# Two of the first branch's projections with tokens on the partitions, the compressed-key product in one rounded pass, and four warming products left out

## The chip, the cores and the metric

One core of a Trainium2 chip runs the whole program. The metric is the device time in microseconds (us) of one execution. Three runs of the kernel before gave 501.91, 502.08 and 502.62 us; their median, 502.08 us, is the time before.

## The reference, cut to what matters

The input x has 256 tokens of 1024 channels. It is normalised and modulated by a vector c (through `w_ada`) into h, and one wide projection `h @ w_in + b_in` feeds three parallel branches, which are mixed by sigmoid gates and projected once more. Cut to the parts that the change touches:

```
proj = h @ w_in[l] + b_in[l]
(aq, ak, av, ao, az, ai, af, ba, bb, bz, cq, ckc, cvc, cks, cvs, ckw, cvw, cg, cz, mg) = split_cols(proj)
# branch a: mLSTM heads over aq, ak, av, then a normalisation per head, and two gates
hf = (hf - mu) * rsqrt(mean((hf - mu)**2) + 1e-5)
hn = hf.reshape(b, s, W_A) * mlstm_norm[l]
y_a = sigmoid(ao) * hn * silu(az)
# branch b: gated causal convolution of 31 taps, layer norm, silu, gate bz
# branch c: attention over three key sets (compressed, selected, window) with gates per head
p_c = masked_softmax(s_c, ...);  o_c = einsum('bgjqn,bngd->bqgjd', p_c, vc)      # 15 compressed blocks
y_c = (gb0 * o_c + gb1 * o_s + gb2 * o_w) * silu(cz)
merged = g0 * (y_a @ w_branch[l, 0]) + g1 * (y_b @ w_branch[l, 1]) + g2 * (y_c @ w_branch[l, 2])
out = x + gate * rmsnorm(merged @ w_out[l], norm_post[l])
```

## The kernel before, in words

All weights are float32 in HBM. For TensorE a float32 operand is split into two rounded parts (`float32r`), hi and lo, and a product becomes three: hi by hi, lo by hi, hi by lo. ScalarE casts the weights to hi (`w_hi`), VectorE subtracts to get lo (`w_lo`); both are in `split` (line 370). Weights come in half megabytes through rings of three hi and three lo tiles and four raw tiles, in the fixed order of the list `order` (line 376); `part` keeps two halves ahead of TensorE. All loads go out on SyncE's queue. Smaller products (attention scores, transposes, attention's products with values) stay in plain float32.

The input projection has two forms. `feat` (line 640) puts output features on the partitions: the weights are the stationary operand, and the 256 tokens the moving one, so that 128 features take 24 products of 256 columns; ScalarE takes each result out with its bias. `tok` (line 660) puts 128 tokens on the partitions: h is stationary, 512 weight columns are the moving operand, and 512 features of 256 tokens take 48 products of 512 columns into two PSUM banks; VectorE takes each result out and adds a bias row that was loaded to all partitions (`vb_av`, `vb_mg`). The kernel before uses `tok` for av, cvs with cvw, and mg, and `feat` for the rest, az and ao among them.

The order of work is written by a planner while the program is built. `Loom` keeps a model clock of each engine and issues every instruction in one program order. Side work is a list of generators (`spawn`, with a rank) that `weave` (line 216) steps between products of the projection when the model says that their operands are ready; `until`, `room`, `slot` and `calm` yield the model time from which a step may go. The 31-tap convolution (`conv_gen`, line 704) is the filler: `weave` issues its VectorE steps only while VectorE's model queue is less than 600 ns ahead of TensorE. `need` forces a generator to its end.

In time: a first wave over the 8 slices of D (lines 515 to 610), whose weights and modulation arrive together; the projections of branch c's keys and queries; per head `h` of four the groups aq, ak, av, az, bz with the head's cell woven in, and the attention (`nsa_gen`, line 1002) woven in across them; then ao and cz; then the branch products c, a, b, each after its mg gates; then the output product.

Attention, per group `g` and token half `t`, ends in a loop (line 1101) that transposes the probabilities in blocks of 128 keys (`flips`), copies them out of PSUM on ScalarE, and multiplies them with the values into one PSUM bank `po`. The compressed keys are the last block: 16 rows of `ptc` (the other 112 are zero) against `vcmp`, one plain float32 product over all 128 rows. Branch a ends in `hnorm_gen` (line 1163): VectorE scales the head's output (`num`, tokens on partitions), TensorE transposes it into `ps_ht`, VectorE multiplies by the gate `ga` (features on partitions, silu(az) times sigmoid(ao) times `anorm`), and `ysplit` (line 772) makes hi on ScalarE and lo on VectorE.

`heat` (line 325) multiplies a tile of ones with itself for no result; `HEAT` gives 10 such products at the start and 4 just ahead of the first wave (line 562).

Of the kernel before, what the change touches and what calls it, by code (L numbers as in the profile page):

```python
# [17 lines left out]
S = 256  # L18
D = 1024
# [16 lines left out]
VROW = ("av", "cv", "mg")  # L36
COLS = dict(av=("av",), cv=("cvs", "cvw"), mg=("mg",))

ORDER = [(n, 0) for n in ("ckc", "cvc", "cks", "ckw")] + [("cv", 0), ("cv", 1)] + [("cq", i) for i in range(4)]
for _i in range(H_A):  # L40
    ORDER += [("aq", _i), ("ak", _i)]
    if _i % 2 == 0:
        ORDER += [("av", _i), ("av", _i + 1)]
    ORDER += [("az", _i), ("bz", _i)]
# [4 lines left out]
VB_MG = 1024 + 512 + N_MISC  # L49

# [13 lines left out]
HEAT = (10, 4)  # L64
# [212 lines left out]
def trunk(ctx: ExitStack, tc, xtok, wada, wave0, wgrp, wmisc, w1, wbr, wout, par, vbias, out):  # L277
# [98 lines left out]
    order = []  # L376
    for n, i in ORDER:
        if n != "mg":
            order.append(("wgrp", (GROUP[n, i],), 2, 1))
# [437 lines left out]
    vcmp = [const.tile([128, 128], F32, name=f"vcmp{g}") for g in range(2)]  # L817
    for g in range(2):
        pool.memset(vcmp[g], 0.0)

    def cmp_gen(j):
# [59 lines left out]
        else:  # L881
            for g in range(2):
# [5 lines left out]
                act.copy(vcmp[g][0:16, :], ps[0:16, 0:128])  # L888
# [113 lines left out]
    def nsa_gen(qs, oc, ptc):  # L1002
        for g in range(2):
            for t in range(2):
# [74 lines left out]
                yield from loom.slot("sd", 2)  # L1079
                po = bank("ps_o", "sd")  # L1080
# [4 lines left out]
                def flips(c, kind, kt):  # L1085
# [6 lines left out]
                    if kind == 2:  # L1092
                        act.copy(ptc[0:16, :], pt[0:16, :])
                        drop(pt)
                        return vcmp[g], ptc
# [4 lines left out]

                ops = yield from flips(*blocks[0])
                for b in range(len(blocks)):
                    v, p_t = ops
                    if b + 1 < len(blocks):
                        ops = yield from flips(*blocks[b + 1])
                    yield until("pe", p_t)
                    mm(po, v, p_t, b == 0, b == len(blocks) - 1)
# [55 lines left out]
    def hnorm_gen(num, ga):  # L1163
# [10 lines left out]
        dve.tensor_tensor(f, f, v3, op=OP.mult)  # L1174
        for h in range(4):
            for t in range(2):
                hn = num[:, 2 * h + t]
                dve.tensor_scalar(hn, hn, mv[:, h, t, 0:1], f[:, h, t:t + 1], op0=OP.subtract, op1=OP.mult)
            yield until("pe", num)
# [5 lines left out]
            gg = ga[:, 2 * h:2 * h + 2]  # L1185
            yield until("dve", pt)
            dve.tensor_tensor(gg, pt.rearrange("p (i q) -> p i q", i=2), gg, op=OP.mult)
# [26 lines left out]
    ptc = const.tile([128, 512], F32, name="ptc")  # L1214
    pool.memset(ptc, 0.0)
# [9 lines left out]
    def silu_gen(h, *deps):  # L1225
        yield from loom.after(*deps)
        for z in (ga, zb):
            if h < 3:
                yield from loom.calm("act", z[:, 2 * h:2 * h + 2])
            act.activation(z[:, 2 * h:2 * h + 2], z[:, 2 * h:2 * h + 2], AF.Silu)  # L1230
# [3 lines left out]
    ga = bigt("ga")  # L1234
    zb = bigt("zb")
    for h in range(4):
# [21 lines left out]
        group_feat("az", h, evac_fn(lambda t: ga[:, t]))  # L1258
# [5 lines left out]
    def gated(t, s, y, scale=None):  # L1264
        if y is ga:
            yield from loom.after(*g_silu)
        yield until("dve", s)
        if scale is None:
            dve.tensor_tensor(y[:, t], y[:, t], s, op=OP.mult)
        else:  # L1270
            dve.scalar_tensor_tensor(y[:, t], y[:, t], scale, s, op0=OP.mult, op1=OP.mult)
# [4 lines left out]
    def evac_cz(t, ps, b):  # L1276
# [4 lines left out]
        late_.append(spawn(gated(t, s, oc), 1))  # L1281

    def evac_ao(t, ps, b):
        if len(late_) > 1:
            need(late_[-2])
        s = ringt(work, [128, S], "sz", "t256", 2)
        act.activation(s, ps, AF.Sigmoid, bias=b)
        late_.append(spawn(gated(t, s, ga, pc("anorm", t)), 1))

    for i in range(4):  # L1290
        group_feat("ao", i, evac_ao)
# [3 lines left out]
    def split_c():  # L1295
        for k in range(0, KT, 2):
            while len(late_) < 10 + k:
                yield loom.now() + 300
            yield from loom.after(*late_[8 + k:10 + k])
# [13 lines left out]
    def branch_a():  # L1313
# [3 lines left out]
        for k in range(0, KT, 2):  # L1317
            yield from ysplit(ga, y_hi, y_lo, k)
# [140 lines left out]
def pack(x, c, w_ada, b_ada, norm_pre, norm_post, w_in, b_in, mlstm_conv_w, mlstm_conv_b, mlstm_norm, conf_dw_w,  # L1459
# [71 lines left out]
    rows = [b_in[OFF[n]:OFF[n] + SIZES[n]] for n in ("av", "cvs", "cvw")] + [bm, b_in[OFF["mg"]:OFF["mg"] + SIZES["mg"]]]  # L1531
# [17 lines left out]
```

## Time and profile before

| | us |
|---|---|
| median of three runs | 502.08 |
| profiled execution, its own time | 502.75 |
| its span, first to last instruction | 501.0 |
| TensorE products / VectorE / ScalarE busy in it | 491.0 / 431.8 / 303.1 |

The profiled execution took 502.75 us, of which 1.75 us lie outside its span. Busy times are of instructions as recorded, and a product is recorded from its issue until its pipeline is through, so that neighbouring products overlap; the share of busy time of TensorE says how rarely it had nothing in hand, and the chain of waits gives the time per product. Nearly all instructions carry line 174, the line of the helper that records them, and so are told apart by their tiles. TensorE's clock was granted in full (1.00) in every stretch up to 494 us.

### The profile page before, as it was taken

What the parts mean: (1) busy time and instruction counts of PE and PEld (TensorE: products, weight loads), DVE (VectorE), ACT (ScalarE), POOL (GpSimd) and SP (SyncE); (2) the same over time, 40 slices, a digit from 0 to 9 for tenths busy, and PEclk for the clock granted to TensorE, in tenths of its full rate; (3) what the DMA queues carried; (4) which work ended last, traced back from release to release, by engine and by line L of the source; (5) the groups of instructions that cost most, each with busy time, mean ns of one, the idle gap of its engine ahead of it and who ended that gap; (6) DMA issues with size and microseconds to landing.
All of it is one profiled execution on the core that took longest, in us unless ns stands there. A gap on an engine that the chain in (4) does not pass through costs nothing.

```text
span 501.0 us, 8523 instructions
## 1 busy us (share of the span) xinstructions
PE 491.0 (98%) x3237; PEld 436.4 (87%) x3237; DVE 431.8 (86%) x871; ACT 303.1 (61%) x519; POOL 7.3 (1%) x41
## 2 busy tenths in 40 slices
PE   8999999999999999999999999999999999999994
PEld 8999998799878989978899799997888788888883
DVE  4989899999999899999999996679998986656745
ACT  6556756245464975977749775666656844454442
POOL 5000000000000000000000000000000000000000
PEclk9999999999999999999999999999999999999998
DMA  8999964884776262232424426554387686655402
GB/s 297 409 359 375 406 244 150 318 352 146 284 285 238 95 241 86 96 156 86 169 84 169 169 84 219 194 208 179 96 317 291 200 354 236 243 220 186 169 0 84
DMA packets 18784, 106.38 MB, mean 212 GB/s; under 512 B 2220, under 2 KB 2616, under 8 KB 8632
## 3 DMA queue, kind: packets, MB, share of 16 engines
q1 hardware_dynamic: 18600, 105.82, 56.0%
q8 instruction: 25, 0.41, 0.3%
q14 instruction: 15, 0.12, 0.1%
q10 hardware_dynamic: 144, 0.03, 0.0%
HBM read 104.78 MB, written 1.06 MB: 211 GB/s over the span
## 4 chain that ended last, share of the span: by engine, by line
PE 83%; DVE 11%; DMA 2%; issue 2%; ACT 1%; SPq 0%; DVEq 0%; ACTq 0%
PE ps_f L174 30%; PE ps_t L174 28%; PE w L174 9%; PE ps_out L174 4%; DVE w_lo L174 4%; DVE acc L174 3%; PE ps_o L174 3%; PE ps_s L174 2%; PE ps_p L174 1%; DMA a_raw<-in_wada_dram 1%; DMA w_raw<-in_w_dram 1%; PE ps_qk L174 1%; PE ps_n L174 1%; PE ps_c L174 1%; DVE cm L174 1%
## 5 line engine op out<-in xcount | busy, mean ns | idle before, releaser
L174 DVE TENSOR_TENSOR w_lo<-w_raw,w_hi 128x1024 fp32r<-128x1024 f32 (+1 forms) x150 | 180.0, 1205 | 40.6 <-ACT w_hi L174 39.2
L174 ACT CAST w_hi<-w_raw 128x1024 fp32r<-128x1024 f32 (+1 forms) x150 | 154.9, 1034 | 81.9 <-PE ps_t L174 53.3
L174 PE MATMUL ps_f<-h_hi,w_hi 128*128 128x256 f32 x512 | 130.7, 291 | 0.0
L174 PE MATMUL ps_f<-h_lo,w_hi 128*128 128x256 f32 x512 | 126.3, 283 | 0.0
L174 PEld LDWEIGHTS ps_f<-h_hi,w_hi 128*128 128x128 f32 x512 | 98.0, 191 | 2.5 <-issue 2.0
L174 PEld LDWEIGHTS ps_f<-h_lo,w_hi 128*128 128x128 f32 x512 | 98.1, 192 | 1.4 <-issue 1.0
L174 DVE SCALAR_TENSOR_TENSOR acc<-u,p_sb,acc 128x226 f32<-128x226 f32 (+28 forms) x232 | 93.0, 460 | 1.8 <-ACT acc L174 1.6
L174 PE MATMUL ps_f<-h_hi,w_lo 128*128 128x256 f32 x512 | 75.7, 288 | 0.0
L174 PEld LDWEIGHTS ps_f<-h_hi,w_lo 128*128 128x128 f32 x512 | 67.0, 191 | 2.6 <-issue 1.9
L174 PE MATMUL ps_t<-w_hi,h_hi 128*128 128x512 f32 x144 | 58.2, 404 | 0.2 <-DVE gs L174 0.2
L174 PE MATMUL ps_t<-w_hi,h_lo 128*128 128x512 f32 x144 | 56.2, 391 | 0.0
L174 PE MATMUL ps_t<-w_lo,h_hi 128*128 128x512 f32 x144 | 44.8, 392 | 0.0
L174 PEld LDWEIGHTS ps_t<-w_hi,h_hi 128*128 128x128 f32 x144 | 27.1, 188 | 6.3 <-DVE gs L174 0.7
L174 PEld LDWEIGHTS ps_t<-w_lo,h_hi 128*128 128x128 f32 x144 | 26.8, 188 | 6.4 <-issue 0.8
L174 PEld LDWEIGHTS ps_t<-w_hi,h_lo 128*128 128x128 f32 x144 | 27.1, 188 | 5.2 <-issue 0.2
L174 PE MATMUL w<-h_lo,w_hi 128*128 128x256 f32 x128 | 31.5, 284 | 0.0
L174 PE MATMUL w<-h_hi,w_lo 128*128 128x256 f32 x128 | 31.4, 283 | 0.0
L174 DVE SCALAR_TENSOR_TENSOR a_raw<-a_raw,cb 128x1024 f32<-128x1024 f32 x23 | 27.4, 1218 | 0.2 <-DMA a_raw<-in_wada_dram 0.2
L174 ACT ACT_TABLE_LOAD x20 | 25.7, 1283 | 1.5 <-PEq L1541 1.2
L174 PEld LDWEIGHTS w<-h_lo,w_hi 128*128 128x128 f32 x128 | 24.5, 191 | 0.1
L174 PEld LDWEIGHTS w<-h_hi,w_lo 128*128 128x128 f32 x128 | 24.5, 192 | 0.0
L174 ACT ACTIVATE pm<-pm,mx 128x16 f32<-128x16 f32 (+2 forms) x48 | 19.0, 400 | 1.9 <-DVE mx L174 1.9
(265 smaller groups left out, 695.5 us busy)
## 6 DMA issues: line engine op xcount, KB each, us to landing
w_raw<-in_wgrp_dram SPq DMA_DIRECT2D x50, 1024.0 KB, 4.9
w_raw<-in_wbr_dram SPq DMA_DIRECT2D x12, 1024.0 KB, 4.8
a_raw<-in_wada_dram SPq DMA_DIRECT2D x16, 512.0 KB, 7.7
w_raw<-in_w_dram SPq DMA_DIRECT2D x8, 1024.0 KB, 4.9
w_raw<-in_wave_dram SPq DMA_DIRECT2D x14, 512.0 KB, 7.0
a_raw<-in_wada_dram SPq DMA_DIRECT2D x4, 1024.0 KB, 4.9
w_raw<-in_wout_dram SPq DMA_DIRECT2D x4, 1024.0 KB, 4.8
vb_mg<-in_vbias_dram SPq DMA_DIRECT2D x3, 512.0 KB, 5.6
```

Source lines behind the costliest of these rows:

```text
L174: inst = self.pin(fn(*args, **kw))
```

## The change

az and ao join the projections with tokens on the partitions: az as two groups, in the passes h = 1 and h = 3, and ao as two groups ahead of cz. Their bias rows are two more loads of 512 KB to all partitions, in the ring of two that holds `vb_av` and `vb_mg`. VectorE now takes both out of PSUM. The gate `ga` is kept with tokens on the partitions, so that in `hnorm_gen` the scaling goes to ScalarE (with a bias `nb`, minus mean times factor) and the gate is multiplied ahead of the transposes; behind them, `hsplit_gen` has ScalarE scale by `anorm` and round to hi, and VectorE form lo, both out of PSUM.

`ptc` and `vcmp` become `float32r` with three bands of 16 rows: hi, lo, hi of the probabilities against hi, hi, lo of the values, so that one rounded product of 512 columns gives the sum of three. The block is transposed first and multiplied last, and the bank `po` is taken only at the first product.

`HEAT`'s second number is 0: the four products ahead of the first wave are left out.

```diff
@@ -33,20 +33,24 @@
-VROW = ("av", "cv", "mg")
-COLS = dict(av=("av",), cv=("cvs", "cvw"), mg=("mg",))
+VROW = ("av", "cv", "az", "ao", "mg")
+COLS = dict(av=("av",), cv=("cvs", "cvw"), az=("az",), ao=("ao",), mg=("mg",))
-    ORDER += [("az", _i), ("bz", _i)]
+    else:
+        ORDER += [("az", _i - 1), ("az", _i)]
+    ORDER += [("bz", _i)]
+VB_AZ = VB_MG + 3 * D
+VB_AO = VB_AZ + D
@@ -61,7 +65,7 @@
-HEAT = (10, 4)
+HEAT = (10, 0)
@@ -374,7 +378,16 @@
+    vb_a = {}
+
+    def load_vb_a(n):
+        vb_a[n] = vbt("vb_" + n)
+        at = VB_AZ if n == "az" else VB_AO
+        loom.load(nc.sync, vb_a[n], vbias[:, at:at + D].broadcast_to([128, D]))
+
+        if n in ("az", "ao") and i == 0:
+            order.append(lambda n=n: load_vb_a(n))
@@ -814,9 +827,9 @@
-    vcmp = [const.tile([128, 128], F32, name=f"vcmp{g}") for g in range(2)]
+    vcmp = [const.tile([128, 128], F32R, name=f"vcmp{g}") for g in range(2)]
-        pool.memset(vcmp[g], 0.0)
+        pool.memset(vcmp[g].bitcast(F32), 0.0)
@@ -885,7 +898,10 @@
-                act.copy(vcmp[g][0:16, :], ps[0:16, 0:128])
+                for q in (0, 32):
+                    act.copy(vcmp[g][q:q + 16, :], ps[0:16, 0:128])
+                yield until("dve", vcmp[g])
+                dve.tensor_tensor(vcmp[g][64:80, :], ps[0:16, 0:128], vcmp[g][0:16, :], op=OP.subtract)
@@ -1076,8 +1092,6 @@
-                yield from loom.slot("sd", 2)
-                po = bank("ps_o", "sd")
@@ -1090,7 +1104,10 @@
-                        act.copy(ptc[0:16, :], pt[0:16, :])
+                        for q in (0, 64):
+                            act.copy(ptc[q:q + 16, :], pt[0:16, :])
+                        yield until("dve", ptc)
+                        dve.tensor_tensor(ptc[32:48, :], pt[0:16, :], ptc[0:16, :], op=OP.subtract)
@@ -1098,13 +1115,19 @@
+                last = yield from flips(*blocks.pop())
-                for b in range(len(blocks)):
+                for b in range(len(blocks) + 1):
+                    else:
+                        ops = last
-                    mm(po, v, p_t, b == 0, b == len(blocks) - 1)
+                    if b == 0:
+                        yield from loom.slot("sd")
+                        po = bank("ps_o", "sd")
+                    mm(po, v, p_t, b == 0, b == len(blocks))
@@ -1172,19 +1195,32 @@
+        nb = work.tile([128, 4, 2], F32, name="hb_", tag="hb_", bufs=1)
+        dve.scalar_tensor_tensor(nb, mv[:, :, :, 0], -1.0, f, op0=OP.mult, op1=OP.mult)
+        yield until("act", nb)
-                dve.tensor_scalar(hn, hn, mv[:, h, t, 0:1], f[:, h, t:t + 1], op0=OP.subtract, op1=OP.mult)
-            yield until("pe", num)
+                act.activation(hn, hn, AF.Identity, scale=f[:, h, t:t + 1], bias=nb[:, h, t:t + 1])
+            hn = num[:, 2 * h:2 * h + 2]
+            yield until("dve", hn)
+            dve.tensor_tensor(hn, hn, ga[:, :, 256 * h:256 * h + 256], op=OP.mult)
+
+    def hsplit_gen(num, y_hi, y_lo):
+        for h in range(4):
+            yield until("pe", num[:, 2 * h:2 * h + 2])
-            gg = ga[:, 2 * h:2 * h + 2]
-            yield until("dve", pt)
-            dve.tensor_tensor(gg, pt.rearrange("p (i q) -> p i q", i=2), gg, op=OP.mult)
+            yield until("act", pt)
+            for i in range(2):
+                act.mul(y_hi[:, 2 * h + i], pt[:, 256 * i:256 * i + 256], pc("anorm", 2 * h + i))
+            yield until("dve", y_hi[:, 2 * h:2 * h + 2])
+            for i in range(2):
+                dve.scalar_tensor_tensor(y_lo[:, 2 * h + i], pt[:, 256 * i:256 * i + 256], pc("anorm", 2 * h + i),
+                                         y_hi[:, 2 * h + i], op0=OP.mult, op1=OP.subtract)
@@ -1211,8 +1247,8 @@
-    ptc = const.tile([128, 512], F32, name="ptc")
-    pool.memset(ptc, 0.0)
+    ptc = const.tile([128, 512], F32R, name="ptc")
+    pool.memset(ptc.bitcast(F32), 0.0)
@@ -1224,14 +1260,14 @@
-        for z in (ga, zb):
+        for z in [zb[:, 2 * h:2 * h + 2]] + ([ga[:, t, 256 * h - 256:256 * h + 256] for t in range(2)] if h % 2 else []):
-                yield from loom.calm("act", z[:, 2 * h:2 * h + 2])
-            act.activation(z[:, 2 * h:2 * h + 2], z[:, 2 * h:2 * h + 2], AF.Silu)
+                yield from loom.calm("act", z)
+            act.activation(z, z, AF.Silu)
-    ga = bigt("ga")
+    ga = bigt("ga", shape=[128, 2, D])
@@ -1255,20 +1291,21 @@
-        group_feat("az", h, evac_fn(lambda t: ga[:, t]))
+        if h % 2:
+            def evac_az(t, ps):
+                w_ = slice(256 * h - 256, 256 * h + 256)
+                dve.tensor_tensor(ga[:, t, w_], ps, vb_a["az"][:, w_], op=OP.add)
+
+            group_tok("az", h // 2, evac_az)
-    def gated(t, s, y, scale=None):
-        if y is ga:
-            yield from loom.after(*g_silu)
+    def gated(s, y, *deps):
+        yield from loom.after(*deps)
-        if scale is None:
-            dve.tensor_tensor(y[:, t], y[:, t], s, op=OP.mult)
-        else:
-            dve.scalar_tensor_tensor(y[:, t], y[:, t], scale, s, op0=OP.mult, op1=OP.mult)
+        dve.tensor_tensor(y, y, s, op=OP.mult)
@@ -1278,25 +1315,30 @@
-        late_.append(spawn(gated(t, s, oc), 1))
-
-    def evac_ao(t, ps, b):
-        if len(late_) > 1:
-            need(late_[-2])
-        s = ringt(work, [128, S], "sz", "t256", 2)
-        act.activation(s, ps, AF.Sigmoid, bias=b)
-        late_.append(spawn(gated(t, s, ga, pc("anorm", t)), 1))
-
-    for i in range(4):
-        group_feat("ao", i, evac_ao)
+        late_.append(spawn(gated(s, oc[:, t]), 1))
+
+    def ao_gate(s, y):
+        yield until("act", s)
+        act.activation(s, s, AF.Sigmoid)
+        yield from gated(s, y, *g_silu)
+
+    for c in range(2):
+        sao = midt("sao", [128, 2, 512])
+
+        def evac_ao(t, ps):
+            w_ = slice(512 * c, 512 * c + 512)
+            dve.tensor_tensor(sao[:, t], ps, vb_a["ao"][:, w_], op=OP.add)
+            late_.append(spawn(ao_gate(sao[:, t], ga[:, t, w_]), 1))
+
+        group_tok("ao", c, evac_ao)
-            while len(late_) < 10 + k:
+            while len(late_) < 6 + k:
-            yield from loom.after(*late_[8 + k:10 + k])
+            yield from loom.after(*late_[4 + k:6 + k])
@@ -1314,8 +1356,7 @@
-        for k in range(0, KT, 2):
-            yield from ysplit(ga, y_hi, y_lo, k)
+        yield from hsplit_gen(num, y_hi, y_lo)
@@ -1529,6 +1570,7 @@
+    rows += [b_in[OFF[n]:OFF[n] + SIZES[n]] for n in ("az", "ao")]
```

## Rows read from the trace of the kernel before

**Rows 1.** Page, part 1: TensorE's busy time, share of the span, instructions.
```profile
PE 491.0 (98%) x3237; PEld 436.4 (87%) x3237; DVE 431.8 (86%) x871; ACT 303.1 (61%) x519; POOL 7.3 (1%) x41
```

**Rows 2.** Chain of waits in order of time: start, us, what, products in it.
```profile
12.73 35.26 PE w L174 x288
...
295.87 38.89 PE ps_f L174 x324
...
416.88 44.48 PE ps_t L174 x196
```

**Rows 3.** Waits, the longest of a weight load after 10 us on another engine.
```profile
PEld ps_t L174 <- DVE w_lo L174: 0.7, 1, 0.7
```

**Rows 4.** Stretches: us; PE, PEld, DVE, ACT, POOL busy (instructions); PEclk, DMA share, GB/s.
```profile
13.00:60.00 47.00, 46.96 (x385) 46.28 (x384) 42.40 (x80) 27.91 (x40) 0.00 (x0) 1.00 1.00 387
60.00:290.00 230.00, 229.45 (x1691) 204.21 (x1690) 223.85 (x551) 150.19 (x311) 0.92 (x9) 1.00 0.50 188
290.00:335.00 45.00, 45.00 (x371) 44.79 (x370) 32.64 (x51) 27.63 (x43) 0.00 (x0) 1.00 0.47 176
335.00:400.00 65.00, 64.44 (x294) 52.80 (x294) 61.49 (x94) 45.37 (x58) 0.00 (x0) 1.00 0.59 220
...
494.00:501.00 7.00, 0.00 (x0) 0.00 (x0) 2.73 (x7) 0.81 (x4) 0.00 (x0) 0.68 0.31 113
```

**Rows 5.** Timeline of TensorE around one product with the compressed values.
```profile
250.12 1.02 PE L174 MATMUL ps_o<-ptc,vcmp 128*128 128x512 f32 x2
250.57 0.68 PE L174 MATMUL ps_f<-h_hi,w_hi 128*128 128x256 f32 x1
251.09 0.28 PE L174 MATMUL ps_f<-h_lo,w_hi 128*128 128x256 f32 x1
```

**Rows 6.** Groups by shape: busy us, mean ns | idle before; the operations' prices.
```profile
L174 DVE TENSOR_TENSOR gs<-ps_t,vb_mg 128x512 f32<-128x512 f32 x12 | 8.1, 683 | 0.5 <-PE ps_t L174 0.5
L174 ACT ACTIVATE sz<-ps_f,p_sb 128x256 f32<-128x256 f32 x16 | 7.6, 476 | 17.3 <-PE ps_f L174 17.3
L174 ACT ACTIVATE h_f<-xn,bcol,acol 128x256 f32<-128x256 f32 x8 | 4.7, 591 | 0.8 <-DVE bcol L174 0.8
L174 DVE SCALAR_TENSOR_TENSOR ga<-ga,p_sb,sz 128x256 f32<-128x256 f32 x8 | 3.8, 478 | 2.9 <-ACT sz L174 2.9
L174 DVE TENSOR_SCALAR num<-num,mv,hf__4122 128x256 f32<-128x256 f32 x8 | 2.9, 403 | 0.0
L174 DVE TENSOR_TENSOR zb<-zb,u 128x512 f32<-128x512 f32 x4 | 2.8, 690 | 0.4 <-ACT u L174 0.4
L174 DVE TENSOR_TENSOR ga<-ps_ht,ga 128x512 f32<-128x512 f32 x4 | 2.7, 681 | 0.2 <-PE ps_ht L174 0.2
L174 DVE TENSOR_TENSOR ya_lo<-ga,ya_hi 128x512 fp32r<-128x512 f32 x4 | 2.6, 681 | 0.0
L174 ACT COPY ptc<-ps_p 16x512 f32<-16x512 f32 x4 | 2.3, 570 | 1.4 <-PE ps_p L174 1.4
```

**Rows 7.** Timeline of the first wave's start, and of ScalarE at its sixth slice.
```profile
11.30 0.41 DVE L174 TENSOR_SCALAR h_hi<-xn,acol,bcol 128x256 fp32r<-128x256 f32 x1
11.68 1.06 PE L174 MATMUL ps_heat<-ones 128*128 128x128 f32 x8
12.49 1.20 PE L174 MATMUL w<-h_hi,w_hi 128*128 128x256 f32 x8
...
40.22 1.05 ACT L174 CAST w_hi<-w_raw 128x1024 fp32r<-128x1024 f32 x1 [0.22 <-DMA w_raw<-in_wave_dram]
```

**Rows 8.** Page, part 6: loads of a bias row: KB each, median us to landing.
```profile
vb_mg<-in_vbias_dram SPq DMA_DIRECT2D x3, 512.0 KB, 5.6
```

**Rows 9.** Timeline of VectorE: the convolution's last two steps.
```profile
298.88 0.88 DVE L174 SCALAR_TENSOR_TENSOR u<-u,p_sb,acc 128x256 f32<-128x256 f32 x2
```

**Rows 10.** Tile yb_lo: ns min/median/max, first and last start of its users.
```profile
L174 PE MATMUL ps_t<-w_hi,yb_lo x32: 388/389/397, 448.3 to 470.0; 128*128 128x512 f32 x32
L174 DVE TENSOR_TENSOR yb_lo<-zb,yb_hi x4: 681/686/686, 388.3 to 401.8; 128x512 fp32r<-128x512 f32 x4
```

## The prediction

> **What bounds the kernel now.** Read the page's busy times first: TensorE has something in hand for 491.0 of 501.0 us, VectorE for 431.8 [rows 1]. That alone doesn't say that TensorE sets the time, since recorded products overlap. So read the chain of waits next, for the time per product: 324 products of 256 columns in 38.89 us are 120.0 ns each, 196 of 512 columns in 44.48 us are 226.9 ns each, and the first wave's 288 take 122.4 ns each [rows 2]. These are steady rates, and the first wave is hardly off them. Then the waits: after the start, the longest of a weight load on another engine is 0.7 us, once [rows 3]. Then the stretches: from 60 to 290 us VectorE is busy 223.85 of 230 us, from 290 to 335 us 32.64 of 45, from 335 to 400 us 61.49 of 65 [rows 4]. A VectorE that full could be the bound, but much of it is the filler, the convolution, whose last step is at 298.88 us [rows 9] and which the planner lets in only where VectorE's queue is short. So: TensorE's own work is the time from 12.5 us on, VectorE stands right behind it, and ScalarE (27.63 of 45, 45.37 of 65 us) has room.
>
> **az and ao on tokens.** Removed: 1024 features each, 16 tiles of 128, times 24, are 384 products of 256 columns, at 120.0 ns 46.1 us. Added: four groups of 48, 192 products of 512 columns, at 226.9 ns 43.6 us. The columns are the same; each pair saves 2 x 120.0 - 226.9 = 13.1 ns, 2.5 us in all, on TensorE, in a stretch where nothing else covers it. For TensorE this is the trace's own price for both forms, and its bounds are narrow: 2.0 to 2.8 us, by 0.5 us that the plain products woven in may cost differently.
>
> The Trainium skill ("TensorE: Matmul & The Clock Gate", section "Back-to-back issue gap") gives the gap of an isolated product as columns over 2.4 GHz plus about 2.5 ns. By it the pair would save only those 2.5 ns, about 0.5 us over 192 pairs, an estimate from that page. The trace differs: 13.3 ns above the column time for both shapes (106.7 and 213.3 ns) [rows 2], and the sum goes by the trace.
>
> What it costs elsewhere. VectorE takes eight results of 512 columns out of PSUM with a bias, at 683 ns 5.5 us; of the ao gate, eight products at 478 ns become four at about 690 ns, -1.1 us [rows 6]. ScalarE loses sixteen passes of 476 ns and gains four sigmoids of 512 columns. Two more bias rows of 512 KB land in 5.6 us [rows 8]; they stand on SyncE's queue ahead of one raw weight load each. The first needs no freed buffer; the second waits for `vb_av`, whose last reader is in pass h = 2, while az, bz and ao are still to come. DMA is busy half of that stretch (0.50, 0.47) [rows 4] and four raw tiles stand ahead, so I take nothing; uncovered, a load late by one landing would cost up to 5.6 us. The ao tiles take two slots of the ring that holds `vtok` and `mspread`; the second must wait for one of them, and the heads' last use of `mspread` is ahead of ao in program order. Nothing again.
>
> **The compressed product.** In plain float32 it starts at 250.12 us as two records; the next product starts behind the first half at 250.57, and the one behind that at 251.09. From 250.12 to 251.09 us are 0.97 us, in which one 256-column product (0.12 us) is done; 0.85 us is the plain product [rows 5]. Rounded, it is one of 512 columns, 227 ns. Four of them (two groups, two halves): 4 x (0.85 - 0.23) = 2.5 us, all on TensorE. Above that, a rounded product between rounded ones may save a change of kind; bounds 2.3 to 3.0 us. Added are four copies of 16 x 512 on ScalarE at 570 ns and four subtractions on VectorE. The trace has none of 16 rows; by the 128-row ones of 512 columns (681 ns) at most 2.7 us, at least 0, and I take 2.7, the row of the same width. The small `vcmp` bands add under 0.5 us. They hide, because the block is now transposed first and multiplied last: two to four other blocks lie between, and a late `ptc` would hold up one product of attention, not the projection.
>
> **Gates and transposes of branch a.** VectorE loses eight scalings (403 ns), four products out of PSUM (681) and four lo subtractions (681), 8.7 us; it gains four gate products (690) and eight lo passes of 256 columns out of PSUM (by the nearest row 478 ns), 6.6 us: -2.1 us. ScalarE gains eight scalings with factor and bias (591) and eight passes out of PSUM (476), 8.5 us, and loses four casts that I leave in [rows 6]. In 335 to 400 us it would be busy 54 of 65 us: hidden, and uncovered it would delay branch a's operand, which is read only after branch c's products. TensorE has the same 16 transposes. Zero, bounds -0.4 to +0.5 us, the one by the wait for VectorE that falls there [rows 3] and the other by one cast of weights that comes late.
>
> **The warming products.** They hold TensorE from 11.68 us until the wave's first product at 12.49. That product's operand is ready at 11.30 + 0.41 = 11.71 us, so at most 0.78 us comes free [rows 7]. But DMA is busy without pause (1.00, 387 GB/s) from 13 to 60 us [rows 4], and at 40.22 us ScalarE still waits for weights to land [rows 7]: an earlier start is largely met by the same landings. I take 0.2 us, bounds 0 to 0.8.
>
> **Sum.** 2.5 + 2.5 + 0 + 0.2 = 5.2 us. The profiled execution's own 502.75 us (501.0 of span) becomes 497.5; the median lies 0.67 us under it, so 496.9 us. In percent of 502.08 that is 1.0.
>
> What is late next is VectorE. Up to 335 us it gains 5.5 - 1.1 + 2.7 + 0.5 = 7.6 us of work while the stretch gets 5.0 us shorter. Its idle time there is 6.15 us (60 to 290) and 12.36 us (290 to 335), 18.5 together [rows 4]; 12.6 of it goes. That the work can move is the convolution's doing: it ends some 20 to 30 us later by the order of the work, ahead of the layer norm at about 330 us. Behind that there is more room: branch b's operand is done at 402 us, and is first multiplied at 448 [rows 10].
>
> **Rivals.**
>
> *Half is given back.* The gain on TensorE is real, but the order that the planner writes anew has VectorE's evacuations of two banks at a time queue behind convolution steps and casts, and some of the groups wait. For it: VectorE at 97% from 60 to 290 us. Against it: the kernel before runs there at the same share with a longest wait of 0.7 us. Four new groups and four attention tails, each with one such wait of 0.3 us (half of that longest), are 2.4 us: 499.3 us. Likewise if a product's fixed cost were a fifth of the 13.3 ns that the rows show, so that the pairs save 0.5 us and not 2.5: 498.9 us; the rows leave that little chance, and it is within these 0.19. That is what the rule of the Trainium skill's page above would make of it.
>
> *More.* All 0.8 us of the warming products, 0.4 us of waits that a lighter VectorE saves after 335 us and 0.5 us of changes of kind: 1.5 us more, 495.4 us.
>
> *Slower: VectorE is the bound.* If the convolution can't give way, what is added on VectorE between 60 and 290 us (half of az's and ao's passes, 2.7, and 3.2 for the bands: 5.9 us) lengthens the stretch, and TensorE's gain there becomes waiting: 508 us. It decides from the point where more than the 6.15 us of idle time in that stretch is asked for, and the convolution's rest no longer fits ahead of 330 us. For it: 5.9 us added and 4 us of shorter stretch exceed 6.15. Against it: the 12.36 idle us behind, and 46 us until branch b's operand is read.
>
> *Slower: the warming products did what they were for.* TensorE's clock is full in every stretch but the last, where it does nothing and 0.68 is granted [rows 4]; so it does fall with idleness. Without the four, TensorE idles only some 0.1 us ahead of the wave. If the clock fell to half for one slice of the wave (48 products, 5.8 us) that slice would take 5.8 us more, and the rest of the sum remains: about 502.9 us, slower by 0.2%.
>
> **How the numbers follow.** Forecast 0.62 (495.9 to 498.2, its terms' bounds); half given back 0.19; more 0.07; VectorE the bound 0.06; the clock 0.03; a late bias row or slot (up to 5.6 us back, about the time before) 0.03. A measurement of this kernel tells 0.2%, 1.0 us, from no change. Faster than that: the forecast, more, and nearly all of half given back, 0.88. Within it: the late load and a little of the others, 0.04. Slower 0.08. The range from 494.8 to 500.2 us leaves out both slower cases, the late load and the far end of each side, together under 2 in 10.
>
> **What would show it.** The steps are right if the profile after has 1152 feature-form products in place of 1536 (64 tiles of 128 features times 24, now 48), at 120 ns, and 192 more of the token form at 227; if `ps_o` of the compressed block is four records, not eight, with some 0.23 us each; if TensorE still waits for no engine longer than 1 us after the start; if the convolution's last step moves from 299 to between 305 and 330 us; and if the wave starts near 11.8 us but ends less than 0.8 us earlier. The prediction is wrong if weight loads wait on `w_lo` or on evacuations of az and ao, if the layer norm waits for the convolution, or if the granted clock ahead of 20 us is below 1.00.

## The result, and the profile after

The changed kernel takes 498.16 us (median of 4 runs, 497.82 to 500.18) against 502.23 us before in the same comparison (501.91 to 502.62): a ratio of 0.9926, 95% interval 0.9909 to 0.9943. That is 4.1 us between the medians, 0.8%, where 5.2 us were forecast, and 498.16 lies in the range. By the interval of the ratio the gain is 2.9 to 4.6 us. A later comparison of the same kernel gave a median of 499.49 us, because its executions lie on two levels ("What stays open"). Between the two profiled executions it is 4.93 us (502.75 to 497.82 us).

The page's busy line, which answers to [rows 1]: TensorE has 204 records fewer (192 of az and ao, 4 of the compressed product, 8 of the warming products) and 5.0 us less busy time, in a span 4.9 us shorter. VectorE has 3.9 us more.

```profile
PE 486.0 (98%) x3033; PEld 424.6 (86%) x3033; DVE 435.7 (88%) x878; ACT 306.7 (62%) x525; POOL 7.3 (1%) x41
```

The chain of waits in order of time (start, us, what, products in it), against [rows 2]. The long pieces give the time per product: 12.00 us over 100 features are 120.0 ns, 44.48 over 196 token products 226.9 ns, as before. The first wave's pieces are now joined, 47.31 us over 384, 123.2 ns each.

```profile
11.63 47.31 PE w L178 x384
58.94 12.00 PE ps_f L178 x100
...
283.46 1.94 PE ps_o L178 x5
...
412.12 44.48 PE ps_t L178 x196
```

The product groups by shape (busy us, mean ns | idle before). Feature products come in three combinations of `h` and `w`, 384 of each, which are the 1152 that were forecast. The token form has 3 x 208 in place of 3 x 144 (the last line is of the kernel before), the forecast 192 more. The means here count records that overlap; the time per product is the chain's.

```profile
L178 PE MATMUL ps_f<-h_hi,w_hi 128*128 128x256 f32 x384 | 96.7, 288 | 0.0
L178 PE MATMUL ps_t<-w_hi,h_hi 128*128 128x512 f32 x208 | 84.2, 405 | 0.0
...
L174 PE MATMUL ps_t<-w_hi,h_hi 128*128 128x512 f32 x144 | 58.2, 404 | 0.2 <-DVE gs L174 0.2
```

The timeline of TensorE around the compressed product (start, us, what), against [rows 5]. Four plain records (two products), then the rounded one, then a token product at 285.24: from start to start 1.94 us, as the chain has it above. Two plain products at 0.85 us are 1.70, and 0.24 us is left for the rounded one.

```profile
283.30 1.88 PE L178 MATMUL ps_o<-p_t,vtok 128*128 128x512 f32 x4
284.61 0.79 PE L178 MATMUL ps_o<-ptc,vcmp 128*128 128x512 f32 x1
285.24 0.39 PE L178 MATMUL ps_t<-w_hi,h_hi 128*128 128x512 f32 x1
```

The stretches (us, then busy time and instructions of TensorE, its weight loads, VectorE, ScalarE and GpSimd, granted clock, DMA share, GB/s), against [rows 4]. VectorE did the new work, yet from 60 to 290 us it is busy 219.27 us where it was 223.85; from 290 to 335 us it is 44.68 of 45 where it was 32.64. So the convolution moved there: 194 of its 232 steps on `acc` start ahead of 290 us, where it was 222, and its last two steps start at 333.63 us, not at 298.88 [rows 9]. The granted clock is full in these stretches.

```profile
6.00:13.00 7.00, 6.91 (x58) 6.45 (x57) 5.83 (x18) 6.17 (x13) 1.01 (x4) 1.00 1.00 381
13.00:60.00 47.00, 47.00 (x386) 46.34 (x385) 43.38 (x84) 29.06 (x41) 0.00 (x0) 1.00 1.02 393
60.00:290.00 230.00, 229.12 (x1589) 200.05 (x1588) 219.27 (x531) 151.02 (x311) 0.92 (x9) 1.00 0.51 191
290.00:335.00 45.00, 45.00 (x290) 41.19 (x290) 44.68 (x88) 29.32 (x42) 0.00 (x0) 1.00 0.55 198
335.00:400.00 65.00, 64.19 (x294) 52.65 (x293) 61.55 (x85) 47.15 (x66) 0.00 (x0) 1.00 0.63 232
```

The waits of weight loads (total us, times, longest): the longest on `w_lo`, in [rows 3] 0.7 us once, is now 1.0, and loads for the compression's products wait three times, 1.4 us in all. Before (the last two lines), they waited once for 0.4 us; and a wait of 0.7 us on a gate's evacuation (`gs`), which stood beside the one in [rows 3], is gone.

```profile
PEld ps_t L178 <- DVE w_lo L178: 1.6, 2, 1.0
...
PEld ps_c L178 <- DMA w_raw<-in_w_dram: 1.4, 3, 0.7
...
PEld ps_c L174 <- DMA w_raw<-in_w_dram: 0.4, 1, 0.4
PEld ps_t L174 <- DVE gs L174: 0.7, 1, 0.7
```

That 1.0 us stands at the first mixing gates. TensorE's timeline (in brackets the idle time before, and what ended it): products come every 0.227 us, then the one on `w_lo` starts 1.00 us behind the last, 0.77 us late. The last line is its weight load, ahead of which the weight loads stood idle for 1.03 us.

```profile
338.28 0.39 PE L178 MATMUL ps_t<-w_hi,h_hi 128*128 128x512 f32 x1
338.50 0.39 PE L178 MATMUL ps_t<-w_hi,h_lo 128*128 128x512 f32 x1
339.50 0.73 PE L178 MATMUL ps_t<-w_lo,h_hi 128*128 128x512 f32 x2 [0.60 <-DVE w_lo L178]
...
339.50 0.30 PEld L178 LDWEIGHTS ps_t<-w_lo,h_hi 128*128 128x128 f32 x2 [1.03 <-DVE w_lo L178]
```

VectorE's timeline says why. The convolution's last steps (`u`) end at 334.5; the layer norm's sums (`lsum`), three additions that the planner issues in one go, run from 335.31 to 337.71; `w_lo` comes behind them and one `yc_lo`.

```profile
333.63 0.88 DVE L178 SCALAR_TENSOR_TENSOR u<-u,p_sb,acc 128x256 f32<-128x256 f32 x2
...
335.31 1.22 DVE L178 TENSOR_TENSOR lsum<-u 128x1024 f32<-128x1024 f32 x1
336.56 1.15 DVE L178 TENSOR_TENSOR lsum<-lsum 128x512 f32<-128x512 f32 x2
337.63 0.68 DVE L178 TENSOR_TENSOR yc_lo<-oc,yc_hi 128x512 fp32r<-128x512 f32 x1
338.23 3.49 DVE L178 TENSOR_TENSOR w_lo<-w_raw,w_hi 128x1024 fp32r<-128x1024 f32 x3
```

The prices of the added work by shape, against [rows 6]: the results of 512 columns out of PSUM 682, the subtraction in 16 rows 680, the ScalarE passes 575, 588 and 464, the `ya_lo` passes 475 ns. Each is within 15 ns of the row by which it was estimated.

```profile
L178 DVE TENSOR_TENSOR ga<-ps_t,vb_az 128x512 f32<-128x512 f32 x4 | 2.7, 682 | 0.0
L178 DVE TENSOR_TENSOR ptc<-ps_p,ptc 16x512 fp32r<-16x512 f32 x4 | 2.7, 680 | 0.1
L178 ACT CAST ptc<-ps_p 16x512 fp32r<-16x512 f32 x8 | 4.6, 575 | 3.8 <-PE ps_p L178 3.7
L178 ACT ACTIVATE num<-num,hb__3958,hf__3918 128x256 f32<-128x256 f32 x8 | 4.1, 588 | 0.0
L178 ACT ACTIVATE ya_hi<-ps_ht,p_sb 128x256 fp32r<-128x256 f32 x8 | 3.3, 464 | 2.5 <-PE ps_ht L178 2.5
L178 DVE SCALAR_TENSOR_TENSOR ya_lo<-ps_ht,p_sb,ya_hi 128x256 fp32r<-128x256 f32 x8 | 3.5, 475 | 0.0
```

The start, TensorE's timeline. With no warming products between, the wave starts at 11.63 us, against 12.49 in [rows 7].

```profile
10.29 1.26 PE L178 MATMUL ps_x<-ident,x_sb 128*128 128x128 f32 x10
11.63 1.19 PE L178 MATMUL w<-h_hi,w_hi 128*128 128x256 f32 x8
```

### The profile page after: what moved, and what is told of

Its sections match the earlier page's. It is cut to its first block, busy times and chain, and to the rows that moved or that the text cites. A ratio compares the mean times of both kernels' runs of the same rounds, so it can differ in the third digit from the quotient of the medians.

```text
span 496.1 us, 8138 instructions
## 1 busy us (share of the span) xinstructions
PE 486.0 (98%) x3033; PEld 424.6 (86%) x3033; DVE 435.7 (88%) x878; ACT 306.7 (62%) x525; POOL 7.3 (1%) x41
## 4 chain that ended last, share of the span: by engine, by line
PE 84%; DVE 11%; DMA 2%; issue 1%; ACT 0%; DVEq 0%; POOL 0%; POOLq 0%
PE ps_t L178 38%; PE ps_f L178 19%; PE w L178 10%; PE ps_out L178 4%; DVE w_lo L178 4%; DVE acc L178 3%; DMA w_raw<-in_w_dram 2%; PE ps_o L178 2%; PE ps_s L178 2%; PE ps_c L178 2%; PE ps_p L178 1%; PE ps_qk L178 1%; PE ps_n L178 1%; PE ps_heat L178 1%; DVE ckb L178 1%
## 5 line engine op out<-in xcount | busy, mean ns | idle before, releaser
L178 PE MATMUL ps_f<-h_hi,w_hi 128*128 128x256 f32 x384 | 96.7, 288 | 0.0
L178 PE MATMUL ps_f<-h_lo,w_hi 128*128 128x256 f32 x384 | 94.5, 283 | 0.0
L178 PE MATMUL ps_t<-w_hi,h_hi 128*128 128x512 f32 x208 | 84.2, 405 | 0.0
L178 PE MATMUL ps_t<-w_hi,h_lo 128*128 128x512 f32 x208 | 81.2, 390 | 0.0
L178 PEld LDWEIGHTS ps_f<-h_hi,w_hi 128*128 128x128 f32 x384 | 73.4, 191 | 1.5 <-issue 1.0
L178 PEld LDWEIGHTS ps_f<-h_lo,w_hi 128*128 128x128 f32 x384 | 73.5, 191 | 0.5
L178 PE MATMUL ps_t<-w_lo,h_hi 128*128 128x512 f32 x208 | 65.6, 397 | 0.6 <-DVE w_lo L178 0.6
L178 PE MATMUL ps_f<-h_hi,w_lo 128*128 128x256 f32 x384 | 56.7, 286 | 0.0
L178 PEld LDWEIGHTS ps_f<-h_hi,w_lo 128*128 128x128 f32 x384 | 50.4, 191 | 1.6 <-issue 0.9
L178 PEld LDWEIGHTS ps_t<-w_hi,h_hi 128*128 128x128 f32 x208 | 39.1, 188 | 8.8 <-issue 1.3
```

Source lines behind the costliest of these rows:

```text
L178: inst = self.pin(fn(*args, **kw))
```

## The experiments

Below, "waits" are my own sums from TensorE's timeline behind the first wave: for each of the larger gaps, the time by which a product starts later than the spacing of its neighbours (120 or 227 ns) asks, added up. They are good to some 0.3 us. The kernel before has 1.3 us of them, the changed one 2.0.

### The parts by themselves

*h_only*: the kernel before, without the last four warming products.

```
-HEAT = (10, 4)
+HEAT = (10, 0)
```

> The kernel before with the four warming products ahead of the first wave left out, nothing else. Theory 1 (the step of the prediction): the first wave is paced by its landings, so that an earlier start is met by the same waits: 0.2 us less, 502.0 us, and the wave's end (first product of the feature form) moves by less than 0.3 us. Theory 2 (read from the trace after, where that end moved by 0.86 us): TensorE paces the wave itself, and all of the products' 0.8 to 0.9 us comes free: 501.4 us. Rival: the clock falls in the wave, over 502.5 us.

*b_only*: the kernel before with the compressed product rounded and multiplied last.

```
-    vcmp = [const.tile([128, 128], F32, name=f"vcmp{g}") for g in range(2)]
+    vcmp = [const.tile([128, 128], F32R, name=f"vcmp{g}") for g in range(2)]
...
+                        dve.tensor_tensor(ptc[32:48, :], pt[0:16, :], ptc[0:16, :], op=OP.subtract)
...
+                last = yield from flips(*blocks.pop())
```

> The kernel before with the compressed keys as one rounded product, transposed first and multiplied last; az, ao, the gates and the warming products as before. Theory 1: four products of 0.85 us become four of 0.23 us on TensorE: 2.5 us less, 499.7 us. Rival: the added copies and subtractions in each attention tail hold products up, half given back: 501.0 us.

*a_only*: the kernel before with az and ao on tokens and branch a's gates.

```
-VROW = ("av", "cv", "mg")
+VROW = ("av", "cv", "az", "ao", "mg")
...
-        group_feat("az", h, evac_fn(lambda t: ga[:, t]))
+            group_tok("az", h // 2, evac_az)
```

> The kernel before with az and ao on tokens and the new gates of branch a; compressed product and warming products as before. Theory 1: 192 pairs save 13.1 ns each: 2.5 us less, 499.7 us. Theory 2: VectorE has the added passes and the convolution moves against the layer norm, so that a wait of some 0.8 us appears ahead of the first mixing gates: 500.5 us. Rival by the page's rule: 0.5 us less, 501.7 us.

*no_h*: the changed kernel with the four warming products back.

```
-HEAT = (10, 0)
+HEAT = (10, 4)
```

> The kernel after with the four warming products put back. Theory 1 (0.2 us of them): 498.4 us. Theory 2 (all of them, 0.8 to 0.9 us): 499.0 us.

Measured on one chip, beside 502.38 us for the kernel before. The last three columns are from the profiled executions: the first product of the wave, the time from the first projection product behind the wave to the end of the span, and the waits. The last row is the changed kernel's first profile; its time is given above.

| kernel | us | ratio (95%) | wave starts | wave to end | waits |
|---|---|---|---|---|---|
| before | 502.38 | 1 | 12.49 | 441.37 | 1.3 |
| h_only | 502.08 | 1.0 (0.9991 to 1.0009) | 11.76 | 440.88 | 0.9 |
| b_only | 501.01 | 0.9974 (0.9965 to 0.9983) | 12.54 | 439.69 | 2.2 |
| a_only | 501.04 | 0.9974 (0.9964 to 0.9984) | 12.92 | 440.63 | 2.7 |
| no_h | 498.78 | 0.9931 (0.9919 to 0.9943) | 12.19 | 437.06 | 1.7 |
| after | | | 11.63 | 437.32 | 2.0 |

The times of the parts don't simply add up. Tokens and compressed product bring 1.3 and 1.4 us alone, 2.7 by addition, and 3.6 us together; the difference of 0.9 us is about as large as the uncertainty of the three intervals together. Each should save 2.5 us of TensorE's content, and each alone gives about 1.1 us back, in the profiles mostly in waits: 441.37 - 2.5 + 0.9 = 439.8 for b_only (439.69 seen), 441.37 - 2.5 + 1.4 = 440.3 for a_only (440.63 seen). With the waits taken off, the content does add up: it is 441.37 - 440.63 + 1.4 = 2.1 us less in a_only, 441.37 - 439.69 + 0.9 = 2.6 in b_only, and 441.37 - 437.06 + 0.4 = 4.7 in no_h.

Neither part's waits stand where its rivals expected them. b_only came out at its rival's 501.0 us, but the waits in its profile are at loads for the compression, at a product of the heads (`ps_n`, 0.4 us) and, as before, at the mixing gates and at `w_lo`, not in the attention tails. In a_only the wait ahead of the first mixing gates is missing: the convolution's last two steps start at 313.81 us there and at 310.10 in b_only; only both parts together push them to 333.63. One of a_only's waits, in TensorE's timeline: branch a's first mixing product waits until VectorE has taken the gates before it out of PSUM.

```profile
393.72 0.50 PE L178 MATMUL ps_t<-w_hi,ya_hi 128*128 128x512 f32 x1 [0.79 <-DVE gs L178]
```

In the changed kernel, where both parts were planned together, 0.4 us is left near that place, on `w_lo`. The warming products are worth 0.3 us alone, within the interval of nothing, though the wave starts 0.7 us earlier in the profile. Over all fourteen profiles the start varied between 12.2 and 12.9 us with them and between 11.6 and 12.0 without; the wave's end varied between 59.1 and 60.0 us with them and between 58.8 and 59.4 without.

### Is the wait behind the layer norm's sums worth its 0.8 us?

*after_again*: the changed kernel, once more, for its own spread.

> The kernel after once more, beside the runs below on the same chip, for an interval: 497.9 to 498.5 us, 4.0 us less than before. Its trace shows again one wait of 0.7 to 0.8 us at the first mixing gates (the third half of weights behind the layer norm's sums).

*after_lsum*: the three sums let in one at a time, each only where VectorE's model queue is short.

```
+        yield loom.room("dve")
         dve.tensor_tensor(a, u[:, 0:4, 1:], u[:, 4:8, 1:], op=OP.add)
-        fold(a)
+        yield loom.room("dve")
+        dve.tensor_tensor(a[:, 0:2], a[:, 0:2], a[:, 2:4], op=OP.add)
+        yield loom.room("dve")
+        dve.tensor_tensor(a[:, 0], a[:, 0], a[:, 1], op=OP.add)
```

> The kernel after with the layer norm's three sums let in one by one, each when VectorE's model queue is less than 900 ns ahead of TensorE's clock, and not all three at once. Theory 2 (the convolution, pushed to the end of the projections, puts the sums ahead of a cast's second half that TensorE then waits for): the wait of 0.77 us goes, 497.5 us. Rival (the wait is only the place where a lag of VectorE comes out): it turns up again a few us later, 498.2 us.

*after_cut*, and *before_cut* as its control: some of the convolution's steps on VectorE are left out, to make room.

```
         for s in range(taps - 1, 1, -1):
+            if taps == CONF_K and s % 6 == 0:
+                continue
```

> The kernel after with 5 of the convolution's 31 taps left out, 40 of 232 steps of about 0.4 us, 16 us of VectorE's work. Theory 2 (VectorE's work is what stands behind TensorE now): the convolution ends ahead of 320 us, the wait of 0.77 us goes, 497.4 us. Theory 1 (VectorE has room and the waits come from the planner's order elsewhere): 498.2 us. If VectorE were the bound all along: 490 us or less.

> The kernel before with the same 5 taps left out, the control to the run above: all theories expect no change, 502.4 us within 0.3; if VectorE set the pace before, 490 us or less.

Measured beside 502.37 us for the kernel before: after_again 499.49 (497.99 to 500.88; ratio 0.9946, 0.9928 to 0.9965), after_lsum 500.65 (498.38 to 501.26; 0.9954, 0.9939 to 0.9970), after_cut 498.78 (498.30 to 499.55; 0.9930, 0.9918 to 0.9942), before_cut 501.90 (501.44 to 502.59; 0.9991, 0.9982 to 0.9999).

In the profiled execution of after_lsum the 0.77 us wait is gone, and so is the one at 394 us; but a gate's evacuation now stands behind `w_lo`, and the next product waits for its bank. TensorE's timeline: 1.56 us from start to start, of which two products are 0.45, so 1.1 us of wait. That execution took 498.38 us, the lowest of the eight, and 437.01 us from the wave to its end, no less than the changed kernel's 437.01 to 437.32 in its three profiles. Five of the eight took 500.6 to 501.3 us and set the median; this wait does not account for them.

```profile
341.72 0.61 PE L178 MATMUL ps_t<-w_lo,h_hi 128*128 128x512 f32 x2
343.28 0.50 PE L178 MATMUL ps_t<-w_hi,h_hi 128*128 128x512 f32 x1 [0.94 <-DVE gs L178]
```

In after_cut VectorE has 12.6 us less between 290 and 335 us (its stretch below; 44.68 in the changed kernel), the convolution's last step starts at 288.8 us instead of 334.0, and the wait behind the sums is gone. The time does not stand out of the changed kernel's own spread (499.49 us here, 498.16 in the first comparison): TensorE instead waits at 126 us for a compression weight to land, and for 0.3 to 0.6 us at three other places, 3.1 us in all. First its stretch, then its timeline:

```profile
290.00:335.00 45.00, 45.00 (x290) 41.22 (x289) 32.06 (x45) 28.26 (x37) 0.00 (x0) 1.00 0.56 199
```

```profile
127.91 1.07 PE L178 MATMUL ps_c<-w_raw,ckb 128*32 128x256 f32 x16 [1.65 <-DMA w_raw<-in_w_dram]
```

On the kernel before the same cut is worth 0.5 us. So neither kernel is bound by VectorE's amount of work. That the planner's order is what moves the waits about is a reading of the profiles. It fits that leaving out the warming products, which leaves the order of work on TensorE, VectorE and ScalarE as it was (h_only against before, the changed kernel against no_h), brings no new wait on another engine behind the wave, while every edit that brought one had changed that order.

### Waits at the compression's loads

*after_look*: the changed kernel, one profile more. *after_w1*: the compression's products are held back 1.2 us of model time, so that their weights have landed. *no_h_w1*: the same, with the warming products back.

```
-            yield until("pe", w, blk)
+            yield until("pe", w, blk) + 1200
```

> The kernel after once more, for a second kind of trace: of ten executions six took 497.8 to 498.8 us and four 500.2 to 500.9, with nothing between. If this one is of the upper level, its trace shows where 2.3 us more are: one wait of TensorE of about that length (a landing that comes late) or a slower first wave. If it is of the lower level, the same waits as before, 0.8 us at the first mixing gates.

> The kernel after with the planner told to leave 1.2 us more between a landing of the first compression weights and their products. Theory 3 (what is given back lies in waits on these eight loads, whose landings vary by 1 to 3 us from run to run): the waits of 0.36 and 0.48 us go and the upper level of 500.5 us gets rare: median 497.5 us. Rival (the levels come from elsewhere): two levels as before, each at most 0.8 us lower.

> The same with the four warming products put back. If leaving them out is what makes the upper level (none of five executions with them showed it): one level only, 498.2 us.

Measured beside 502.62 us: after_look 498.19 in its one run, with the changed kernel's waits again (0.5 us at 132, 0.8 at 339, 0.4 at 395); after_w1 499.78 (498.57 to 500.03; ratio 0.9938, 0.9924 to 0.9952); no_h_w1 498.70 (498.40 to 500.01; 0.9924, 0.9911 to 0.9937). The held-back products waited no less in after_w1: a new 1.0 us for a load at 152, and 0.9 us on `w_lo` at 218. In no_h_w1 the waits at the compression were gone, one of 0.9 us at 217 was new, and the time is no_h's. Taking a single wait away in this way gained nothing either time. In the four kernels whose convolution ends by 322 us (a_only, after_cut, after_w1, no_h_w1) the wait at 339 us is gone, and waits of 0.2 to 1.0 us stand near 356, 369 and 392 us instead.

after_w1 and no_h_w1 were measured side by side and run the same order, and so do the changed kernel and no_h. In neither pair is the kernel without the warming products shown to be faster: 499.78 against 498.70 us here; 498.16, 499.49 and 498.19 (one run) against 498.78 for no_h.

### The sums on another engine

*pool_sum*: no_h with the layer norm's three additions on GpSimd, which is idle there.

```
-        dve.tensor_tensor(a, u[:, 0:4, 1:], u[:, 4:8, 1:], op=OP.add)
-        fold(a)
-        yield until("pe", a)
+        pool.tensor_tensor(a, u[:, 0:4, 1:], u[:, 4:8, 1:], op=OP.add)
+        pool.tensor_tensor(a[:, 0:2], a[:, 0:2], a[:, 2:4], op=OP.add)
+        pool.tensor_tensor(a[:, 0], a[:, 0], a[:, 1], op=OP.add)
+        yield loom.now() + 10000
```

> The kernel after with the warming products put back and the layer norm's three sums on GpSimd, which is idle there, instead of VectorE; the product that reads them is planned 10 us later. Theory 2 (the sums, pushed against the next casts by the longer convolution, cost the wait of 0.8 us at the first mixing gates): that wait goes and nothing takes its place, 498.0 us, the lowest of all kernels here. Rival (VectorE's lag comes out elsewhere, as when the sums were let in one by one): a wait of 0.5 to 1 us turns up within 15 us behind, 498.8 us as without this edit.

Measured: 500.05 us (499.81 to 500.34; ratio 0.9945, 0.9929 to 0.9961) beside 502.56. no_h had 0.9931 (0.9919 to 0.9943) in another comparison, so by the times alone it is not shown to be slower; in the profiles the stretch from the wave to the end is 1.9 us longer (439.00 against 437.06). The two timelines, GpSimd's and VectorE's: while the first addition runs, from 335.20 to 337.59, a VectorE step on 128x8, 0.17 us just before, takes 2.25 us; while the second runs, a later one takes 1.15; and a `w_lo` step that meets the third takes 1.74 us where it is 1.22 otherwise.

```profile
335.20 2.39 POOL L730 TENSOR_TENSOR lsum<-u 128x1024 f32<-128x1024 f32 x1 [111.09 <-DVE hx__3930 L178]
337.67 1.30 POOL L731 TENSOR_TENSOR lsum<-lsum 128x512 f32<-128x512 f32 x1
339.05 1.14 POOL L732 TENSOR_TENSOR lsum<-lsum 128x256 f32<-128x256 f32 x1
```

```profile
335.16 0.17 DVE L178 SCALAR_TENSOR_TENSOR hx__3930<-hx__3930,hw__3929 128x8 f32<-128x8 f32 x1
335.37 2.25 DVE L178 SCALAR_TENSOR_TENSOR hw__3929<-hx__3930,hw__3929 128x8 f32<-128x8 f32 x1
...
337.85 1.15 DVE L178 SCALAR_TENSOR_TENSOR hb__3962<-mv,hf__3922 128x8 f32<-128x8 f32 x1
...
339.52 1.74 DVE L178 TENSOR_TENSOR w_lo<-w_raw,w_hi 128x1024 fp32r<-128x1024 f32 x1
```

So the work left VectorE and its time didn't: the three steps are 3.6 us longer than without GpSimd's additions, and the sums had taken 2.4 us on VectorE. Counted from the convolution's end, `w_lo` was done 1.3 us later than in the changed kernel, and TensorE's wait grew from 0.81 us in no_h to 2.06: its products start at 339.03 and, in place of 339.26, at 341.32 us. Its clock followed. First TensorE's timeline, then the stretches (the granted clock is the third number from the end):

```profile
339.03 0.39 PE L178 MATMUL ps_t<-w_hi,h_lo 128*128 128x512 f32 x1
341.32 0.73 PE L178 MATMUL ps_t<-w_lo,h_hi 128*128 128x512 f32 x2 [1.90 <-DVE w_lo L178]
```

```profile
336.00:341.00 5.00, 3.42 (x16) 2.49 (x14) 4.93 (x5) 1.96 (x4) 4.03 (x3) 1.00 0.01 3
341.00:346.00 5.00, 4.68 (x15) 3.69 (x16) 5.00 (x8) 4.98 (x10) 0.00 (x0) 0.67 0.70 223
...
343.00:344.00 1.00, 1.00 (x4) 0.81 (x3) 1.00 (x3) 1.00 (x3) 0.00 (x0) 0.50 0.74 311
346.00:347.00 1.00, 1.00 (x7) 0.87 (x6) 1.00 (x2) 1.00 (x1) 0.00 (x0) 0.93 0.46 164
```

## Why the prediction was right, and where it was off

**The sum.** Forecast 5.2 us; between the profiles 4.93, between the medians 4.1, and 2.9 to 4.6 by the interval, so the forecast gain was too large. (The profiled execution of the kernel before lies 0.5 us above its median in that comparison, the changed one's 0.3 below.) In the profiles the wave ends 0.86 us earlier, and from there to the end it is 441.37 - 437.32 = 4.05 us. By content that stretch should have lost 2.5 + 2.5 = 5.0; 0.7 us more waits take it to 4.3, and 0.3 us is not assigned. Two readings in the prediction were off without changing the forecast: its terms' bounds add up to 495.1 to 498.3 us, not 495.9 to 498.2, and the longest wait of a weight load on another engine, 0.7 us, stood there twice, on `w_lo` and on `gs`.

**az and ao on tokens: right in its term.** Both rates stand where they stood, 120.0 and 226.9 ns, and the counts are as forecast. Only 1.34 us reached the time when it was alone; in the profiles its content is 2.1 us less, good to some 0.3. By the gap that the Trainium skill ("TensorE: Matmul & The Clock Gate", "Back-to-back issue gap") gives for an isolated product the pairs would have saved 0.5 us, an estimate from that page. With 1.4 us more waits a_only would then be about 0.9 us slower than before; it was faster (0.9964 to 0.9984). The measurement decides: the trace's prices, 120.0 and 226.9 ns, are the ones to go by here.

**The compressed product: right.** 0.24 us where 0.23 was forecast, four records for eight. The longest wait of a weight load on `ptc` or on an operand of `ps_o` is 0.2 us.

**Branch a's gates: right as a nothing.** The passes cost what the rows said, and the stretch from 335 to 400 us has VectorE at 61.55 us where it was 61.49, ScalarE at 47.15 where 54 was forecast. All sixteen new passes of ScalarE start between 338 and 364 us; the forecast was too high because it left in the four casts that were dropped (613 ns each), and one table load (1.28 us) fewer falls in the stretch. The late bias rows did not come to pass either: az's and ao's rows landed 7.7 and 5.7 us after their issue, where 5.6 was read, and no wait on them is in the profile.

**The warming products: undersized for this profile, not for the time.** 0.2 us was forecast, and less than 0.8 at the wave's end; the profiled wave starts and ends 0.86 us earlier. In the changed kernel's two other profiles, and in h_only's, the start is 0.6 to 0.7 us earlier and the end only 0.3 to 0.4: part is met by the landings, as was argued. So about half of the 0.86 us was luck of that one execution. In h_only's time they are worth 0.3 us, not distinguishable from none, and no run shows that this part of the change gains anything. No clock was lost: it is 1.00 from 6 to 400 us.

**New waits at nothing: the term that was wrong.** The sum took zero for waits that a new order brings. Measured are +0.7 us in the changed kernel's profile, +0.9 in b_only and +1.4 in a_only. The rival "half is given back" named this; its places were wrong (not the new groups and attention tails) and its size, 2.4 us, is larger than any of these. One sign that the prediction had named for being wrong did appear: weight loads wait on `w_lo`, twice, 1.6 us in all, where it was 0.7 us once. The criterion "no engine waited for longer than 1 us" was narrowly missed: the weight load at 339.50 us waited 1.03 us, though its product came only 0.77 us late.

**The convolution's end: mis-sized.** 305 to 330 us was forecast from 7.6 us of new work against idle time; the last two steps start at 333.63. Ahead of 290 us VectorE is busy 4.6 us less than before although it got new work, so the filler was not merely pushed by the new work but let in less often. With the convolution ending at 334.5 us, the layer norm's sums fall ahead of a `w_lo` that TensorE is about to read. VectorE as the bound is refuted all the same: with 40 of 232 steps left out the kernel before gains 0.5 us, and the changed one nothing beyond its spread.

**What stays open.** The 11 executions of the changed kernel lie on two levels: seven from 497.8 to 498.8 us, four from 500.2 to 500.9. All its profiled ones are on the lower, with the same waits but for one of 0.4 us at 97 us, so what the other 2.3 us are is not shown; they are more than half of the gain. They set the median of a comparison: 498.16 us with one of four on the upper level, 499.49 with three of six. With the warming products back, none of five runs was on the upper level (the highest is 499.58), and in no_h_w1 one of five came near it (500.01), which is too few to say that they prevent it. Where b_only's and a_only's waits come from in the planner's order was read from their profiles, not forced by a run. No version tried beats the changed kernel for certain: no_h_w1 at 498.70 and no_h at 498.78 lie within its two levels.

## What to carry to other kernels

Price the bounding engine's own work by the rows of its steady rates: counts and rates came out as forecast even for a shape moved from one form to another, and the content less its waits added up (2.1 and 2.6 us alone, 4.7 together). Then charge an edit of a planned order one or two waits of 0.5 to 1 us: here each part alone lost about 1.1 of 2.5 us, mostly to them, and taking one wait away made another. A change smaller than that can only be judged by its time, and times of parts that were measured separately need not give the whole (2.7 against 3.6 us).

## What the runs showed of the hardware

- In pool_sum VectorE and GpSimd did not run side by side: a 128x8 step of VectorE took 2.25 us while GpSimd added 128x1024 float32 (2.39 us); the same step takes 0.17 us in the changed kernel. The Trainium skill ("SBUF — State Buffer", "Who interferes with whom") calls the port pair of these two an exclusive lock, by which a VectorE operation with two SBUF inputs, issued behind a GpSimd one that reads SBUF, is blocked to its end. The trace agrees: the step ends at 337.62, the addition at 337.59.
- GpSimd's additions took 2.39, 1.30 and 1.14 us for 1024, 512 and 256 columns; VectorE's first of these takes 1.22 us.
- In pool_sum a wait of 2.06 us on TensorE, which ended at 341.32 us, was followed by a fall of its granted clock: 1.00 from 341 to 342 us, 0.50 from 343 to 346, the lower of its two levels (1.2 of 2.4 GHz), with products 0.43 us apart that are 0.227 at full clock, and 1.00 again from 347 us. Behind the changed kernel's 0.77 us wait the granted clock stayed at 1.00 over 335 to 400 us.
